# Unit products from GpSimd to VectorE, and a scratch image of whole 32x32 blocks, in the input projection of a two-layer fp32 block

## The chip, the cores and the metric

One core of one Trainium2 chip runs the whole kernel in one launch. The metric is the device time of that launch in microseconds (us). A number of the profile comes from one profiled execution, whose own time stands in the table below.

## The reference, cut to what matters

Two layers over 1280 tokens (256 of context, 1024 latent), everything in fp32, width 1024. Each layer projects the normalised tokens into 23 groups of 128 columns, mixes them, projects back and ends with a mixture of experts. The part that matters here is the mixing of 8 heads of 64 channels by a recurrence, run in both directions:

```python
kk = kk / jnp.maximum(jnp.sqrt(jnp.sum(kk * kk, axis=-1, keepdims=True)), 1e-12)
...
a = jax.nn.sigmoid(iclr_a0[dn] + la @ iclr_a2[dn])
k_dir = k * (1.0 + (a - 1.0) * k_a)
...
s = (s * d_t[:, :, None, :]
     - s_kk[..., None] * (kk_t * a_t)[:, :, None, :]
     + v_t[..., None] * k_t[:, :, None, :])
```

The kernel runs it in chunks of 64 tokens. Within a chunk and head, the steps depend on each other through a triangular 64x64 matrix with ones on its diagonal, which has to be inverted.

## The kernel before, in words

`inproj` does the projection of a layer and, beside it, everything of the recurrence that does not need the running state. The projection is a stream (`project`): per group of 128 columns three matmuls (L397) for each of 8 pieces of the inner dimension and each strip of tokens. The rest is cut into 16 **units**: a pair of heads (e = 0 and 1, 64 partitions each), a half of the tokens (10 chunks), a direction. Per unit:

- `heads` (every second unit): GpSimd spreads the inverse norms over 64 channels (L480), PE turns them by 5 matmuls with the identity (L484), VectorE multiplies (L485).
- `gates`: PE makes two inputs (L502), ScalarE takes tanh (L506), VectorE maps it to the sigmoid by 0.5x+0.5 (L508), a running sum and two exponentials follow.
- `factors`: products of these. The left operand bk of the next step is half GpSimd's work (partitions 64 to 127, L532 and L533) and half VectorE's (L534, L535); the sum over both directions is GpSimd's (L544, L545).
- `attn`: PE multiplies bk with ar (L561), VectorE masks into X (L566). The 64x64 matrices go to a scratch image gD in DRAM (L578), other parts to scratch for the scan (L573, L575). PE transposes bk (L583), ScalarE copies it (L587), and it goes out as well (L589).
- `inverse`, for 3 units at once: the 120 diagonal 32x32 blocks are loaded from gD, one block to a partition, and inverted in place by GpSimd in 30 steps of a product and a sum (L605, L607). ScalarE then makes the transposed blocks zt (L611; L617 and L621 at the end of the layer), and both are stored, to gD (L612, L618) and xD (L622). Units 12 and 13 are inverted on VectorE.
- `merge`: per unit the block inverses come back from gD (L635) and their transposes from xD (L636), and two rounds of PE (L645, L647) and ScalarE (L652, L654) make the missing corner of the 64x64 inverse; the result is stored (L655).

Order: unit u's turn runs merge(u-6), gates(u), attn(u-1), heads, factors(u); after every third unit an inverse is started whose blocks are finished three units later. The class `Pace` puts projection matmuls behind marked PE instructions (`pace.point`), so that PE has work while other engines prepare a unit; a scheduler then fixes the order on every engine. The last merges of a layer run beside the scan (L1061 is the first matmul of a scan step, with st as its tile). All large DMAs are issued by SP, in one order, and each waits for the one eight issues earlier, since eight semaphores are used in turn. So an issue that waits holds up everything behind it.

Of the kernel before, what the change touches and what calls it, by code (L numbers as in the profile page):

```python
# [47 lines left out]
HT, HC = T // 2, NCH // 2  # L48

Q = 32 * C + 32  # L50
U_ = 2 * Q


# [70 lines left out]
class K:  # L124
# [223 lines left out]
    def inproj(self, l, last):  # L348
# [12 lines left out]
        om = sp.tile([P, 15], F32, name="om")  # L361
        nc.vector.tensor_scalar(om, self.vec("mu", 0, 15), -1.0, 1.0, op0=OP.mult, op1=OP.add)
        oka = sp.tile([P, 4], F32, name="oka")
        nc.vector.tensor_scalar(oka, self.vec("ka", 0, 4), -1.0, 1.0, op0=OP.mult, op1=OP.add)
        wah = sp.tile([P, 2, 8], F32, name="wah")
# [17 lines left out]
        def bank():  # L383
            return bk_[0].tile([P, 1024], F32, name="ps1", bufs=bk_[1])
# [92 lines left out]
        def heads(p, hf, k, inv):  # L477

            kk = un.tile([P, HT], F32, name="kk", bufs=2)
# [36 lines left out]

        def factors(p, hf, d, r, k, kk, g, kds):
# [4 lines left out]
            kd = un.tile([P, HC, C], F32, name="kd", bufs=2)  # L522
            nc.scalar.activation(kd, aa, AF.Identity, bias=oka[:, p:p + 1], scale=self.vec("ka", p))
# [6 lines left out]
            bk = un.tile([P, HC, 2, C], F32, name="bk")  # L530
            lo, hi = slice(0, 64), slice(64, 128)
# [11 lines left out]
            if len(kds) == 2:  # L543
                nc.gpsimd.tensor_tensor(kds[0], kds[0], kds[1], op=OP.add)  # L544
                nc.gpsimd.tensor_tensor(kds[0], kds[0], cv(r, hf), op=OP.mult)  # L545
                nc.sync.dma_start(self.prD[p][:, hf * HT:(hf + 1) * HT], flat(kds[0]))
            return ar, bk

        def attn(p, hf, d, ar, bk):

            GR = ((0, 5), (5, 5))
            half = lambda e: slice(64 * e, 64 * e + 64)
            img = slice(hf * HC, (hf + 1) * HC)

            Xs = [un.tile([P, 2, HC, C], F32, name="X", bufs=2) for _ in range(2)]
            for c0, n in ((0, 4), (4, 3), (7, 3)):
                ps = bank().rearrange("q (e c s t) -> q e c s t", e=2, s=2, t=C)
                for c in range(n):
                    for e in range(2):
                        h = half(e)  # L560
                        mm = nc.tensor.matmul(ps[:, e, c], bk[h, c0 + c].rearrange("q s t -> q (s t)"), ar[h, :, c0 + c, :],  # L561
                                              start=True, stop=True)
# [5 lines left out]
            for e in range(2):  # L568
# [3 lines left out]
                for v, rows in ((ar[h], h), (X[o], o)):  # L572
# [3 lines left out]
                                  X[h, 1].rearrange("q (n c) t -> q n (c t)", c=2))  # L576
                m = (2 * place[p, hf, d] + e) * HC
                nc.sync.dma_start(self.mats(self.gD, m, HC), X[h, 0])  # L578

            for c0, n in GR:  # L580
                ps = bank()
# [5 lines left out]
                nc.scalar.activation(bt[:, :n].rearrange("q c t -> q (c t)"), ps[:, :n * P], AF.Copy)  # L587
                ch = slice(hf * HC + c0, hf * HC + c0 + n)
                nc.sync.dma_start(self.btD[d][ch, :, p, :].rearrange("c q x -> q c x"), bt[:, :n])  # L589

        def inverse(u0, n, eng, new=None):
# [4 lines left out]
            else:  # L596
                gt = new()[:n]
                gt, tmp = gt[:, :1024], gt[:, 1024:1280]
            gt = gt.rearrange("q (i a) -> q i a", a=32)
            nc.sync.dma_start(gt, self.diag(self.gD, j0, n))  # L600
            nc.gpsimd.memset(gt.rearrange("q s t -> q (s t)")[:, 0:1024:33], 1.0)
# [6 lines left out]
            def finish():  # L608
                if new is None:
# [3 lines left out]
                else:  # L613
                    xs = [qp.tile([P, 512], F32, name=name)[:n].rearrange("q (a i) -> q a i", i=32)
                          for name in ("pq", "pl")]
                    for x, sl in zip(xs, (slice(0, 16), slice(16, 32))):
                        nc.scalar.activation(x, gt[:, :, sl].rearrange("q i a -> q a i"), AF.Copy)  # L617
                    nc.sync.dma_start(self.diag(self.gD, j0, n), gt)  # L618
                    xt = gt
                    for x, sl in zip(xs, (slice(0, 16), slice(16, 32))):  # L620
                        nc.scalar.activation(xt[:, sl], x, AF.Copy)  # L621
                nc.sync.dma_start(self.diag(self.xD, j0, n), xt)  # L622
            return finish

        def merge(u, new, bank="pq"):
# [7 lines left out]
            for e, (r, o) in enumerate(ro):  # L633
                m = (2 * u + e) * HC
# [357 lines left out]

    @staticmethod
    def mats(t, m, n):

        return bass.AP(tensor=t.tensor, offset=t.offset + m * U_, ap=[[C, C], [U_, n], [1, C]])

    @staticmethod
    def diag(t, b, n):

        return bass.AP(tensor=t.tensor, offset=t.offset + b * Q, ap=[[Q, n], [C, 32], [1, 32]])

# [827 lines left out]
def trace(tc, a, out):  # L1830
# [17 lines left out]
    k.yD = [dram(f"yD{d}", [2, T, 4 * C]) for d in range(2)]  # L1848
    k.gD = dram("gD", [5 * P * Q])
    k.xD = dram("xD", [5 * P * Q])  # L1850
    xs = [a["x0"], dram("x1", [T, D])]
# [90 lines left out]
```

## Time and profile before

| | us |
|---|---|
| runs: median (lowest to highest of 3) | 3627.87 (3625.42 to 3634.18) |
| the profiled execution: its own time | 3623.64 |
| its span on the core | 3621.7 |
| PE, VectorE (DVE), ScalarE (ACT), GpSimd (POOL) busy in it | 3063.4, 2281.6, 1880.5, 1178.0 |

The units of layer 1 lie between about 160 and 640 us of the span, those of layer 2 between about 2010 and 2490. The chain that ended last covers only the last few microseconds, so the stretch is read through what PE waited for. A line number is that of the kernel before; a name such as zt is the program's name of a tile, and `zt<-xD` a load of it.

### The profile page before, as it was taken

The page shows a single profiled execution, that of the slowest core. Times are in us where ns is not written, and L with a number is a line of the kernel's source. Part 1 is how long each engine was busy: PE and PEld are TensorE (multiplying, and loading weights), DVE is VectorE, ACT ScalarE, POOL GpSimd, SP SyncE. Part 2 cuts the span into 40 slices and gives each one's busy share as a digit, 9 for nine tenths or more (in the row PEclk, how much of TensorE's full clock was granted, in tenths as well). Part 3 has the DMA queues.
Part 4 walks back from the last instruction along what each step waited for, and adds up shares of the span by engine and source line. Part 5 has one row for each costly group of instructions (what it writes and reads, how often), then busy time and mean ns, then how long its engine had stood idle before and what let it go on. Part 6 is the DMA issues. An engine that isn't in the chain of part 4 may idle for free. (4 is left out here: it accounts for less than half of the span.)

```text
span 3621.7 us, 59282 instructions
## 1 busy us (share of the span) xinstructions
PE 3063.4 (85%) x22308; PEld 2426.6 (67%) x22308; DVE 2281.6 (63%) x3543; ACT 1880.5 (52%) x2838; POOL 1178.0 (33%) x1101
## 2 busy tenths in 40 slices
PE   6998788888997999999829988778878978999992
PEld 3776666676686777777616766556666857777772
DVE  4265566134487888888672665652334778888886
ACT  4343433335344777778652434323343467777783
POOL 0037675211221222222140276743113122233323
PEclk8998888899998999999959988778988989999996
DMA  6677888879746899999667578889795488899995
GB/s 241 207 167 173 185 192 181 246 230 315 260 142 243 334 339 338 365 373 363 257 227 258 144 169 181 176 180 252 240 285 167 133 315 317 331 366 364 360 366 205
DMA packets 708060, 922.35 MB, mean 255 GB/s; under 512 B 335074, under 2 KB 561259, under 8 KB 657852
## 3 DMA queue, kind: packets, MB, share of 16 engines
q1 hardware_dynamic: 669456, 871.05, 75.8%
q0 software_dynamic: 38304, 47.49, 3.9%
q8 instruction: 177, 2.90, 0.3%
q14 instruction: 111, 0.91, 0.1%
q10 hardware_dynamic: 12, 0.00, 0.0%
HBM read 726.92 MB, written 203.23 MB: 257 GB/s over the span
## 5 line engine op out<-in xcount | busy, mean ns | idle before, releaser
L176 DVE TENSOR_TENSOR hl<-ld,hl 128x1024 fp32r<-128x1024 f32 x734 | 869.2, 1228 | 54.2 <-ACT hl L175 44.2
L175 ACT ACTIVATE hl<-ld 128x1024 fp32r<-128x1024 f32 x796 | 798.5, 1052 | 38.4 <-PE pR L1571 21.9
L1571 PE MATMUL pR<-hl,wk 128*128 128x512 f32 x1560 | 455.1, 400 | 0.0
L1571 PE MATMUL pU<-hl,wk 128*128 128x512 f32 x1560 | 446.9, 395 | 0.0
L397 PE MATMUL pb<-hh,wh 128*128 128x512 f32 (+1 forms) x1000 | 393.0, 394 | 10.2 <-ACT wh L175 5.4
L397 PE MATMUL pb<-hl,wh 128*128 128x512 f32 (+1 forms) x1000 | 389.1, 390 | 0.0
L397 PE MATMUL pb<-hh,wl 128*128 128x512 f32 (+1 forms) x1000 | 385.4, 386 | 0.0
L1595 PE MATMUL pA<-hl,wk 128*128 128x512 f32 x1560 | 382.9, 401 | 0.5 <-ACT wk L175 0.5
L1571 PEld LDWEIGHTS pU<-hl,wk 128*128 128x128 f32 x1560 | 294.5, 189 | 68.3
L1595 PEld LDWEIGHTS pA<-hl,wk 128*128 128x128 f32 x1560 | 292.7, 191 | 64.0 <-ACT wk L175 0.7
L1571 PEld LDWEIGHTS pR<-hl,wk 128*128 128x128 f32 x1560 | 288.3, 189 | 60.7 <-ACT wk L175 0.3
L176 POOL TENSOR_TENSOR hl<-ld,hl 128x1024 fp32r<-128x1024 f32 x62 | 184.2, 2971 | 422.4 <-ACT hl L175 422.4
L397 PEld LDWEIGHTS pb<-hh,wh 128*128 128x128 f32 x1000 | 200.2, 200 | 76.8 <-issue 14.1
L1602 POOL DMA_INDIRECT yb<-wk,sca x64 | 94.8, 1482 | 468.2 <-ACT wk L1601 452.1
L1276 PE MATMUL pA<-hl,wk 128*128 128x512 f32 x864 | 226.6, 413 | 7.7 <-POOL wk L176 4.0
L397 PEld LDWEIGHTS pb<-hl,wh 128*128 128x128 f32 x1000 | 201.1, 201 | 37.9 <-issue 10.3
L397 PEld LDWEIGHTS pb<-hh,wl 128*128 128x128 f32 x1000 | 200.2, 200 | 35.2 <-issue 4.6
L1100 POOL DMA_DIRECT2D yD<-yt x72 | 58.0, 805 | 433.7 <-ACT yt L1099 391.6
L1276 PEld LDWEIGHTS pA<-hl,wk 128*128 128x128 f32 x864 | 163.0, 195 | 49.2 <-issue 6.0
L1088 DVE TENSOR_TENSOR tm<-pR,ST 128x256 f32<-128x256 f32 x76 | 32.1, 423 | 249.4 <-PE pR L1083 237.4
L175 ACT ACTIVATE wk<-pm 128x256 fp32r<-128x256 f32 (+1 forms) x195 | 88.8, 455 | 185.6 <-PE pm L1586 169.3
L607 POOL TENSOR_TENSOR gt<-gt,tmp 120x30 f32<-120x30 f32 (+14 forms) x240 | 168.3, 701 | 17.7
(425 smaller groups left out, 5389.6 us busy)
## 6 DMA issues: line engine op xcount, KB each, us to landing
ld<-in_exp_gu SPq DMA_DIRECT2D x260, 1024.0 KB
ld<-in_exp_dn SPq DMA_DIRECT2D x130, 1024.0 KB
st<-rlD SPq DMA_DIRECT2D x80, 512.0 KB
wr<-in_w_in SPq DMA_DIRECT2D x46, 512.0 KB
rlD<-ar SPq DMA_DIRECT2D x64, 320.0 KB
rlD<-X SPq DMA_DIRECT2D x64, 320.0 KB
btD<-bt SPq DMA_DIRECT2D x64, 320.0 KB
st<-abD SPq DMA_DIRECT2D x40, 512.0 KB
```

Source lines behind the costliest of these rows:

```text
L175: nc.scalar.activation(hi, src, AF.Copy)
L176: (eng or nc.vector).tensor_tensor(lo, src, hi.bitcast(F32), op=OP.subtract)
L397: mm = nc.tensor.matmul(ps[:, :n], w[:, k, :], h[:, k, c0:c0 + n], start=(k == 0 and i == 0), stop=(k == KD - 1 and i == 2))
L607: eng.tensor_tensor(gt[:, 0:j, j + 1:32], gt[:, 0:j, j + 1:32], tv, op=OP.add)
L1088: nc.vector.tensor_tensor(tm, RS[:, 1], ST[d], op=OP.add)
L1100: nc.gpsimd.dma_start(self.yD[d][:, ch * C:(ch + 1) * C, :], yt.rearrange("q p d -> q (p d)"))
L1276: nc.tensor.matmul(ps, oo[o][:, k, :], w[k][w_][:, fs], start=(k == 0 and q == 0), stop=(k == KD - 1 and q == 2))
L1571: nc.tensor.matmul(o, x.xT[xi][:, kk, :], w[wi][:, k, :], start=(kk == 0 and i == 0), stop=(kk == KD - 1 and i == 2))
L1595: nc.tensor.matmul(x.y[n], x.h[:, hi_, f, :], dw[wi][:, 0, n * 512:(n + 1) * 512], start=(f == 0 and i == 0), stop=(f == 3 and i == 2))
L1602: nc.gpsimd.indirect_dma_start(out=yb, out_offset=bass.IndirectOffsetOnAxis(ap=x.sca, axis=0), in_=o, in_offset=None, bounds_check=2 * T - ...
```

## The change

GpSimd keeps only the block inverses. `heads` broadcasts on PE (10 matmuls instead of 5). In `gates` and `factors` the map 0.5x+0.5 of the second gate is folded into what follows, that of the first goes to ScalarE, and all products go to VectorE. bk has three slots instead of two, so that its product kk*a is one instruction over 128 partitions; the transposition of bk by PE becomes 20 plain matmuls with 64 columns instead of 10 transposes with 128. The image gD holds whole 32x32 blocks (4 KB each, contiguous), and the corner blocks lie in another image, nD: `attn` writes three pieces per e instead of one, `inverse` loads and stores its blocks whole. The transposed image xD is gone, with ScalarE's copies and the store; `merge` loads three pieces per e instead of two, and transposes the blocks by 20 matmuls with the identity (L640 of the new kernel) and two copies, ahead of its two rounds.

```diff
@@ heads
-            nc.gpsimd.tensor_copy(kk.rearrange("q (t e d) -> q t e d", e=2, d=64),
-                                 inv[:, 5 * hf:5 * hf + 5, :, None].to_broadcast([P, 5, 2, 64]))
             for t in range(5):
-                nc.tensor.matmul(ps[:, t * P:(t + 1) * P], kk[:, t * P:(t + 1) * P], self.ident, start=True, stop=True)
+                for e in range(2):
+                    nc.tensor.matmul(ps[64 * e:64 * e + 64, t * P:(t + 1) * P],
+                                     inv[:, 5 * hf + t, e:e + 1].to_broadcast([P, 64]), self.ident, start=True, stop=True)
@@ gates
-                nc.vector.tensor_scalar(dst, dst, 0.5, 0.5, op0=OP.mult, op1=OP.add)
+                if i == 0:
+                    nc.scalar.activation(dst, dst, AF.Copy, bias=0.5, scale=0.5)
@@ factors
-            nc.vector.tensor_tensor(aa, aa, Ei, op=OP.mult)
+            nc.vector.scalar_tensor_tensor(aa, aa, 1.0, Ei, op0=OP.add, op1=OP.mult)
...
-            nc.gpsimd.tensor_tensor(bk[hi, :, 0, :], kd[hi], Ei[hi], op=OP.mult)
-            nc.gpsimd.tensor_tensor(bk[hi, :, 1, :], kk[hi, :, rev], aa[hi, :, rev], op=OP.mult)
-            nc.vector.tensor_tensor(bk[lo, :, 1, :], kd[lo], Ei[lo], op=OP.mult)
-            nc.vector.tensor_tensor(bk[lo, :, 0, :], kk[lo, :, rev], aa[lo, :, rev], op=OP.mult)
+            for e in range(2):
+                h = slice(64 * e, 64 * e + 64)
+                nc.vector.tensor_tensor(bk[h, :, 2 - 2 * e], kd[h], Ei[h], op=OP.mult)
+            nc.vector.scalar_tensor_tensor(bk[:, :, 1], kk[:, :, rev], 0.5, aa[:, :, rev], op0=OP.mult, op1=OP.mult)
...
-                nc.gpsimd.tensor_tensor(kds[0], kds[0], kds[1], op=OP.add)
-                nc.gpsimd.tensor_tensor(kds[0], kds[0], cv(r, hf), op=OP.mult)
+                nc.vector.tensor_tensor(kds[0], kds[0], kds[1], op=OP.add)
+                nc.vector.tensor_tensor(kds[0], kds[0], cv(r, hf), op=OP.mult)
@@ attn
-                nc.sync.dma_start(self.mats(self.gD, m, HC), X[h, 0])
+                for b in range(2):
+                    q = slice(32 * b, 32 * b + 32)
+                    nc.sync.dma_start(self.diag(m, b), X[h, 0][q, :, q])
+                nc.sync.dma_start(self.corner(m), X[h, 0][0:32, :, 32:64])
...
-                    mm = nc.tensor.transpose(ps[:, c * P:(c + 1) * P], bk[:, c0 + c].rearrange("q s t -> q (s t)"),
-                                             self.ident)
+                    for e in range(2):
+                        h = half(e)
+                        mm = nc.tensor.matmul(ps[:, e, c], left(e, c0 + c), self.ident[h, h], start=True, stop=True)
@@ inverse, finish
-                    xt = un.tile([P, 32, 32], F32, name="zt")[:n]
-                    nc.scalar.activation(xt, gt.rearrange("q i a -> q a i"), AF.Copy)
-                    nc.sync.dma_start(self.diag(self.gD, j0, n), gt)
...
-                nc.sync.dma_start(self.diag(self.xD, j0, n), xt)
+                nc.sync.dma_start(img, gt.rearrange("q i a -> q (i a)"))
@@ merge
-                nc.sync.dma_start(AM[64 * e:64 * e + 64], self.mats(self.gD, m, HC))
-                nc.sync.dma_start(XP[r], self.mats(self.xD, m, HC)[lo, :, lo])
+                nc.vector.memset(AM[o, :, lo], 0.0)
+                nc.sync.dma_start(AM[r, :, hi], self.corner(m))
+                for b, (rows, cols) in enumerate(((r, lo), (o, hi))):
+                    nc.sync.dma_start(AM[rows, :, cols], self.diag(m, b))
...
+                            nc.tensor.matmul(pq[r, c, :], AM[r, c, lo], self.ident[r, r], start=True, stop=True)
...
+                    nc.scalar.activation(XP[r], pq[r], AF.Copy)
@@ the image
+    def blocks(self, b, n):
+        return bass.AP(tensor=self.gD.tensor, offset=self.gD.offset + b * 1024, ap=[[1024, n], [1, 1024]])
+    def diag(self, m, b):
+        return bass.AP(tensor=self.gD.tensor, offset=self.gD.offset + (2 * HC * m + b) * 1024,
+                       ap=[[32, 32], [2048, HC], [1, 32]])
+    def corner(self, m):
+        return bass.AP(tensor=self.nD.tensor, offset=self.nD.offset + HC * m * 1024, ap=[[32, 32], [1024, HC], [1, 32]])
```

The order of SP around an early merge of layer 1 before, from the X writes of one unit (gD, rlD, abD) to the loads of the merge (zt):

```order
L578 DMA gD<-X 64x10x64
L573 DMA rlD_62<-X 64x10x128
L575 DMA abD_64<-X 64x5x128
L578 DMA gD<-X 64x10x64
L589 DMA btD_66<-bt 128x5x128
L635 DMA zt<-gD 64x10x64
L636 DMA zt<-xD 32x10x32
L589 DMA btD_66<-bt 128x5x128
L635 DMA zt<-gD 64x10x64
L636 DMA zt<-xD 32x10x32
```

The same place after:

```order
L581 DMA gD<-X 32x10x32
L582 DMA nD<-X 32x10x32
L574 DMA rlD_62<-X 64x10x128
L576 DMA abD_64<-X 64x5x128
L581 DMA gD<-X 32x10x32 x2
L582 DMA nD<-X 32x10x32
L595 DMA btD_66<-bt 128x5x128
L630 DMA zt<-nD 32x10x32
L632 DMA zt<-gD 32x10x32 x2
L595 DMA btD_66<-bt 128x5x128
L630 DMA zt<-nD 32x10x32
L632 DMA zt<-gD 32x10x32 x2
```

Between the first X write and the last load of the merge there are now six more issues: four X writes and two loads.

The order of PE at the first merge of layer 1 before (L397 is the projection, L561 the products of `attn`, L645 and L647 the rounds of the merge):

```order
L397 MATMUL pb<-hh,wl 128x256
L645 MATMUL pq<-zt 32x32
L561 MATMUL ps_2765<-ar,bk 128x128 x8
L645 MATMUL pq<-zt 32x32 x19
L561 MATMUL ps_2776<-ar,bk 128x128 x6
L397 MATMUL pb<-hh,wl 128x512
L397 MATMUL pb<-hh,wh 128x512
L397 MATMUL pb<-hl,wh 128x512
L647 MATMUL pq<-zt 32x32 x20
```

The same merge after, in its two pieces. First the transpositions (L640) and what follows them, where L501 is the unit's gates:

```order
L396 MATMUL pb<-hl,wh 128x512
L640 MATMUL pq<-ident,zt 32x32 x20
L501 MATMUL ps_2860<-lw,w_589 128x320 x2
L501 MATMUL ps_2865<-la,a_590 128x320 x2
L396 MATMUL pb<-hh,wh 128x256
L396 MATMUL pb<-hl,wh 128x256
```

Then, ten projection matmuls later, the first round (L650) with `attn` (L562) behind it:

```order
L396 MATMUL pb<-hh,wh 128x256
L396 MATMUL pb<-hl,wh 128x256
L650 MATMUL pq<-zt 32x32 x20
L562 MATMUL ps_2876<-ar,bk 128x128 x8
L562 MATMUL ps_2887<-ar,bk 128x128 x6
```

Before, the merge's first round stood behind the gates, around the products of `attn`; now the transpositions, which wait for the loads, stand ahead of the gates, and `attn` stands behind the first round.

## Rows read from the trace of the kernel before

**Rows 1.** The page: busy time of the engines; granted TensorE clock in 40 slices.

```profile
PE 3063.4 (85%) x22308; PEld 2426.6 (67%) x22308; DVE 2281.6 (63%) x3543; ACT 1880.5 (52%) x2838; POOL 1178.0 (33%) x1101
...
PEclk8998888899998999999959988778988989999996
```

**Rows 2.** Busy time by window (columns as in the header), units of layers 1 and 2.

```profile
160.00:640.00 480.00, 411.60 (x3214) 329.17 (x3214) 288.19 (x392) 186.75 (x264) 283.41 (x343) 0.88 0.80 176
2010.00:2490.00 480.00, 393.07 (x3024) 305.61 (x3018) 280.76 (x389) 178.10 (x258) 287.82 (x358) 0.84 0.82 180
```

**Rows 3.** Waits of PE, layer 1 (160:640): total us, times, longest us.

```profile
PE pq L645 <- DMA zt<-xD: 30.8, 8, 13.4
PE pR L1061 <- DMA st<-vE: 11.8, 1, 11.8
PE ps L561 <- POOL bk L533: 7.6, 3, 3.7
```

**Rows 4.** Waits of PE, layer 2 (2010:2490).

```profile
PE pq L645 <- DMA zt<-xD: 25.8, 10, 6.7
PE ps L561 <- POOL bk L533: 14.3, 4, 5.8
PE pR L1061 <- DMA st<-vE: 12.3, 2, 12.1
```

**Rows 5.** Timeline of PE: start, duration, work, in brackets the idle time before.

```profile
346.20 0.24 PE L645 MATMUL pq<-zt 32*32 32x32 f32 x2 [4.37 <-DMA zt<-xD]
...
444.91 0.28 PE L645 MATMUL pq<-zt 32*32 32x32 f32 x2 [13.37 <-DMA zt<-xD]
...
606.30 0.28 PE L645 MATMUL pq<-X 32*32 32x32 f32 x2 [4.13 <-DMA X<-xD]
...
2376.87 0.31 PE L645 MATMUL pq<-zt 32*32 32x32 f32 x2 [6.75 <-DMA zt<-xD]
```

**Rows 6.** Groups of POOL by shape, layer 1: busy us, mean ns, idle before.

```profile
L533 POOL TENSOR_TENSOR bk<-kk,aa 64x640 f32<-64x640 f32 x16 | 34.1, 2133 | 2.8 <-DVE kk L485 2.5
L532 POOL TENSOR_TENSOR bk<-kd,Ei 64x640 f32<-64x640 f32 x16 | 32.3, 2016 | 43.6 <-PE ps L583 20.9 <-issue 17.2 <-ACT v L430 3.6
```

**Rows 7.** A product of DVE: its group, and its min/median/max ns in 200:560.

```profile
L534 DVE TENSOR_TENSOR bk<-kd,Ei 64x640 f32<-64x640 f32 x16 | 19.3, 1207 | 21.9 <-PE ps L583 21.7
...
L534 DVE TENSOR_TENSOR bk<-kd,Ei x14: 816/932/2170, 206.4 to 538.9; 64x640 f32<-64x640 f32 x14
```

**Rows 8.** Timeline of PE: three starts, each with the start behind it.

```profile
486.89 0.82 PE L645 MATMUL pq<-zt 32*32 32x32 f32 x40
487.64 0.50 PE L397 MATMUL pb<-hh,wh 128*128 128x512 f32 x1
...
650.00 0.68 PE L1074 MATMUL pU<-RH,st 64*64 64x64 f32 x16
650.61 0.50 PE L397 MATMUL pb<-hh,wl 128*128 128x512 f32 x1
...
357.13 0.71 PE L583 MATMUL ps<-ident,bk 128*128 128x128 f32 x5
357.60 0.48 PE L397 MATMUL pb<-hl,wh 128*128 128x512 f32 x1
```

**Rows 9.** Timeline of SP's queue: start and duration of DMA issues.

```profile
356.54 1.54 SPq L578 DMA_DIRECT2D gD<-X  x1
...
365.49 0.62 SPq L636 DMA_DIRECT2D zt<-xD  x1
366.16 0.64 SPq L635 DMA_DIRECT2D zt<-gD  x1
...
585.17 2.08 SPq L622 DMA_DIRECT2D xD<-zt  x1
587.35 4.03 SPq L573 DMA_DIRECT2D rlD<-X  x1
```

**Rows 10.** The DMA view of 320:340: its packet rows.

```profile
q1 hardware_dynamic: 10606, 2.78, 70.2%
```

More of the change, by code (lines that the diff above doesn't have):

```diff
@@ L48 @@
 HT, HC = T // 2, NCH // 2
-Q = 32 * C + 32
-U_ = 2 * Q
 VOFF = {}
@@ L362, in inproj @@
         nc.vector.tensor_scalar(om, self.vec("mu", 0, 15), -1.0, 1.0, op0=OP.mult, op1=OP.add)
+        hka = sp.tile([P, 4], F32, name="hka")
+        nc.vector.tensor_scalar(hka, self.vec("ka", 0, 4), 0.5, None, op0=OP.mult)
         oka = sp.tile([P, 4], F32, name="oka")
-        nc.vector.tensor_scalar(oka, self.vec("ka", 0, 4), -1.0, 1.0, op0=OP.mult, op1=OP.add)
+        nc.vector.tensor_scalar(oka, self.vec("ka", 0, 4), -0.5, 1.0, op0=OP.mult, op1=OP.add)
         wah = sp.tile([P, 2, 8], F32, name="wah")
@@ L477, in heads @@
         def heads(p, hf, k, inv):
-            kk = un.tile([P, HT], F32, name="kk", bufs=2)
-            nc.gpsimd.tensor_copy(kk.rearrange("q (t e d) -> q t e d", e=2, d=64),
-                                 inv[:, 5 * hf:5 * hf + 5, :, None].to_broadcast([P, 5, 2, 64]))
+            kk = un.tile([P, HT], F32, name="kk")
             ps = bank()
             for t in range(5):
-                nc.tensor.matmul(ps[:, t * P:(t + 1) * P], kk[:, t * P:(t + 1) * P], self.ident, start=True, stop=True)
+                for e in range(2):
+                    nc.tensor.matmul(ps[64 * e:64 * e + 64, t * P:(t + 1) * P],
+                                     inv[:, 5 * hf + t, e:e + 1].to_broadcast([P, 64]), self.ident, start=True, stop=True)
             nc.vector.scalar_tensor_tensor(kk, k[:, hf * HT:(hf + 1) * HT], self.vec("kk", p), ps[:, :HT],
@@ L522, in factors @@
             kd = un.tile([P, HC, C], F32, name="kd", bufs=2)
-            nc.scalar.activation(kd, aa, AF.Identity, bias=oka[:, p:p + 1], scale=self.vec("ka", p))
+            nc.scalar.activation(kd, aa, AF.Identity, bias=oka[:, p:p + 1], scale=hka[:, p:p + 1])
             nc.vector.tensor_tensor(kd, kd, cv(k, hf), op=OP.mult)
             kds.append(kd)
-            nc.vector.tensor_tensor(aa, aa, Ei, op=OP.mult)
+            nc.vector.scalar_tensor_tensor(aa, aa, 1.0, Ei, op0=OP.add, op1=OP.mult)
             ar = un.tile([P, 2, HC, C], F32, name="ar")
-            bk = un.tile([P, HC, 2, C], F32, name="bk")
-            lo, hi = slice(0, 64), slice(64, 128)
-            nc.gpsimd.tensor_tensor(bk[hi, :, 0, :], kd[hi], Ei[hi], op=OP.mult)
-            nc.gpsimd.tensor_tensor(bk[hi, :, 1, :], kk[hi, :, rev], aa[hi, :, rev], op=OP.mult)
-            nc.vector.tensor_tensor(bk[lo, :, 1, :], kd[lo], Ei[lo], op=OP.mult)
-            nc.vector.tensor_tensor(bk[lo, :, 0, :], kk[lo, :, rev], aa[lo, :, rev], op=OP.mult)
+            bk = un.tile([P, HC, 3, C], F32, name="bk")
+            for e in range(2):
+                h = slice(64 * e, 64 * e + 64)
+                nc.vector.tensor_tensor(bk[h, :, 2 - 2 * e], kd[h], Ei[h], op=OP.mult)
+            nc.vector.scalar_tensor_tensor(bk[:, :, 1], kk[:, :, rev], 0.5, aa[:, :, rev], op0=OP.mult, op1=OP.mult)
             if d == 0:
@@ L552, in attn @@
             half = lambda e: slice(64 * e, 64 * e + 64)
+            left = lambda e, c: bk[half(e), c, 1 - e:3 - e].rearrange("q s t -> q (s t)")
             img = slice(hf * HC, (hf + 1) * HC)
@@ L560, in attn @@
                         h = half(e)
-                        mm = nc.tensor.matmul(ps[:, e, c], bk[h, c0 + c].rearrange("q s t -> q (s t)"), ar[h, :, c0 + c, :],
+                        mm = nc.tensor.matmul(ps[:, e, c], left(e, c0 + c), ar[h, :, c0 + c, :],
                                               start=True, stop=True)
@@ L576, in attn @@
                                   X[h, 1].rearrange("q (n c) t -> q n (c t)", c=2))
-                m = (2 * place[p, hf, d] + e) * HC
-                nc.sync.dma_start(self.mats(self.gD, m, HC), X[h, 0])
+                m = 2 * place[p, hf, d] + e
+                for b in range(2):
+                    q = slice(32 * b, 32 * b + 32)
+                    nc.sync.dma_start(self.diag(m, b), X[h, 0][q, :, q])
+                nc.sync.dma_start(self.corner(m), X[h, 0][0:32, :, 32:64])
             for c0, n in GR:
-                ps = bank()
+                ps = bank().rearrange("q (e c d) -> q e c d", e=2, d=C)
                 for c in range(n):
-                    mm = nc.tensor.transpose(ps[:, c * P:(c + 1) * P], bk[:, c0 + c].rearrange("q s t -> q (s t)"),
-                                             self.ident)
+                    for e in range(2):
+                        h = half(e)
+                        mm = nc.tensor.matmul(ps[:, e, c], left(e, c0 + c), self.ident[h, h], start=True, stop=True)
                 pace.point(mm, W_ATTN)
                 bt = un.tile([P, 5, P], F32, name="bt", bufs=2)
-                nc.scalar.activation(bt[:, :n].rearrange("q c t -> q (c t)"), ps[:, :n * P], AF.Copy)
+                nc.scalar.activation(bt[:, :n].rearrange("q c (e d) -> q c e d", e=2),
+                                     ps[:, :, :n].rearrange("q e c d -> q c e d"), AF.Copy)
                 ch = slice(hf * HC + c0, hf * HC + c0 + n)
@@ L598, in inverse @@
                 gt, tmp = gt[:, :1024], gt[:, 1024:1280]
+            img = self.blocks(j0, n)
+            nc.sync.dma_start(gt, img)
             gt = gt.rearrange("q (i a) -> q i a", a=32)
-            nc.sync.dma_start(gt, self.diag(self.gD, j0, n))
             nc.gpsimd.memset(gt.rearrange("q s t -> q (s t)")[:, 0:1024:33], 1.0)
@@ L608, in finish @@
             def finish():
-                if new is None:
-                    xt = un.tile([P, 32, 32], F32, name="zt")[:n]
-                    nc.scalar.activation(xt, gt.rearrange("q i a -> q a i"), AF.Copy)
-                    nc.sync.dma_start(self.diag(self.gD, j0, n), gt)
[L613 to L621, printed above, removed]
-                nc.sync.dma_start(self.diag(self.xD, j0, n), xt)
+                nc.sync.dma_start(img, gt.rearrange("q i a -> q (i a)"))
             return finish
@@ L633, in merge @@
             for e, (r, o) in enumerate(ro):
-                m = (2 * u + e) * HC
-                nc.sync.dma_start(AM[64 * e:64 * e + 64], self.mats(self.gD, m, HC))
-                nc.sync.dma_start(XP[r], self.mats(self.xD, m, HC)[lo, :, lo])
-            def work(ctx):
+                m = 2 * u + e
+                nc.vector.memset(AM[o, :, lo], 0.0)
+                nc.sync.dma_start(AM[r, :, hi], self.corner(m))
+                for b, (rows, cols) in enumerate(((r, lo), (o, hi))):
+                    nc.sync.dma_start(AM[rows, :, cols], self.diag(m, b))
+            def work(ctx):
+                pq = qp.tile([P, 512], F32, name=bank)[:, :HC * 32].rearrange("q (u t) -> q u t", t=32)
+                for c in range(HC):
+                    for r, o in ro:
+                        with ctx:
+                            nc.tensor.matmul(pq[r, c, :], AM[r, c, lo], self.ident[r, r], start=True, stop=True)
+                        ctx = nullcontext()
+                for r, o in ro:
+                    nc.scalar.activation(XP[r], pq[r], AF.Copy)
                 for st in range(2):
@@ L991, in fill @@
         next(tail, None)
[L993 to L1001, printed above, removed]
+    def blocks(self, b, n):
[5 more added lines that the diff above has]
+        return bass.AP(tensor=self.nD.tensor, offset=self.nD.offset + HC * m * 1024, ap=[[32, 32], [1024, HC], [1, 32]])
     def scan(self, l, last):
@@ L1848, in trace @@
     k.yD = [dram(f"yD{d}", [2, T, 4 * C]) for d in range(2)]
-    k.gD = dram("gD", [5 * P * Q])
-    k.xD = dram("xD", [5 * P * Q])
+    k.gD = dram("gD", [64 * HC * 1024])
+    k.nD = dram("nD", [32 * HC * 1024])
     xs = [a["x0"], dram("x1", [T, D])]
```

## The prediction

> **What bounds the kernel now.** I read the page's busy times first. PE is busy 85% of the span, and its granted clock is often 9 or 8 tenths rather than full [rows 1]. An engine that full sets the time of its stretches, but a busy PE at a low clock or a waiting PE still leaves something to win. The change touches the units alone, so I read their two stretches by window: of 480 us in each, PE is busy 411.60 and 393.07, and idle for the other 68 and 87; its clock is 0.88 and 0.84 [rows 2]. VectorE is at 60%, ScalarE at 39%, GpSimd at 59%, and the DMA engines at 80%: none of them is full, and the question is only where one of them ends last.
>
> PE's waits answer it. Most of the idle time is the merge's first round waiting for its last load, 30.8 us in layer 1 and 25.8 in layer 2; then comes the start of the scan, 11.8 and 12.3; GpSimd's half of bk is only 7.6 and 14.3 [rows 3, 4]. Single waits show two kinds of merge wait: four long ones (13.37, 6.75, 4.37, 4.13), which stand where an inverse's blocks go out, and many short ones [rows 5]. Without the three long ones at zt, that is 24.5, the others take 56.6 - 24.5 = 32 us in 15 waits, 2.1 us each. So GpSimd's products have a price of 22 us at most, and the waits beside the inverses' traffic one of 28.6.
>
> **GpSimd's products.** They go: the two largest groups alone are 34.1 and 32.3 us of layer 1 [rows 6]. PE's waits for them, 7.6 + 14.3 = 21.9, can vanish [rows 3, 4]. VectorE is next in the chain, with 64-row products of 1207 ns on average [rows 7] in place of GpSimd's 2016 and 2133 [rows 6], two of them now being in sequence with what it did anyhow. I take three quarters, **-16**, between -22 and 0. VectorE's load grows little: per unit it loses two maps, and gains the second half of one product for bk and one product for the kd sums, while its half of kk*aa grows to 128 rows. With 40% of its time free [rows 2] I cost that at nothing; the same for ScalarE, which gains one map per unit and two small copies per merge, and loses the large transposing copies (61% free). Their cover is PE's stream; if it were gone, each step of a unit would be later by about one product, 1 us, which is inside the bound of 0 above.
>
> First the row: the same product of 64x640 takes 816 ns at best, 932 in the median and 2170 at worst [rows 7], so something outside it stretches it at times. The Trainium skill (SBUF — State Buffer, "Who interferes with whom") says that a VectorE instruction with two SBUF inputs and a GpSimd instruction that reads SBUF share a port, and that the later one waits for the whole of the earlier. By that rule VectorE's products would fall to their 816 ns where GpSimd is silent, and the inverses would take longer beside VectorE's added products. In the sum it would be 16 x (1207 - 816) ns = 6 us per layer on VectorE, which is off the path: nothing by either. No run here shows yet which engine gives way.
>
> **The inverse's traffic.** Gone are the transposed image's store, ScalarE's transposition before it, and the scattered rows of the block load and store. At the end of one inverse the store of xD holds SP's queue 2.08 us, and the next issue 4.03 [rows 9]. In 320:340, a stretch with one such exchange, 10606 packets take 70.2% of 16 engines for 20 us, 21 ns each [rows 10]. Before, an image crosses three times per inverse in rows of 128 bytes, 120 x 32 x 3 = 11520 packets, or 15 us of all 16 engines by these 21 ns; whole blocks need 240 large packets. Of the four long waits (28.6 us [rows 5]) I take **-26**, between -29 and 0.
>
> **The merge's loads.** Between a unit's first X write and the merge's last load, SP issues six more DMAs than before (the order rows above). An issue takes 0.62 to 0.64 us there, for a small piece as for a large one [rows 9]; so the last load can be late by 6 x 0.63 = 3.8 us. Queued behind it on SP are the next unit's stores and the projection's weights. Against this, whole blocks free the engines on which these loads wait. PE's order decides what is seen of it: the transpositions now stand ahead of the gates, and two to four dozen projection matmuls behind the unit before, which cover part. I take **+18**, 1 us for each of 18 merges with zt (9 per layer), between 0 and 18 x 3.8 = +68.
>
> **PE's extra work.** Nearest rows, at full clock: 40 matmuls of 32x32 in 0.75 us (486.89 to 487.64), 16 of 64 columns in 0.61 (0.038 each), 5 of 128 columns in 0.47 (0.094 each) [rows 8]. Per layer: the merge's transpositions, 16 x 0.75 = 12.0; bk's, 16 x (40 x 0.038 - 10 x 0.094) = 9.3, as a plain fp32 matmul runs as two; the broadcast, 8 x 10 x 0.094 = 7.5. That is 29 per layer, 58 in both, and 58 / 0.86 = 67 at the clock of these stretches. It lies in the stretch that PE bounds, but PE idles 155 us there, partly where these small matmuls stand. I take somewhat under a half, **+26**, between 0 and +67.
>
> **The end of a layer.** The last inverses stand ahead of the scan's loads in SP's queue, and PE waits 11.8 and 12.3 us there [rows 3, 4]. With the transposed image gone, I take 5 us of each, **-10**, between -20 and 0.
>
> **The clock.** It fell where PE waited. One hundredth more over the 805 us in which PE is busy [rows 2] is 805 x 0.01 / 0.86 = 9: **-9**, between -20 and +10.
>
> **Sum**: -16 - 26 + 18 + 26 - 10 - 9 = -17. The profiled execution took 3623.6; that makes 3606.6, and the runs' median lies 4.2 above the profiled one: **3611 us**, 0.5% faster. About 0.3% (11 us) is what a measurement of this kernel can tell from no change.
>
> **The rivals.**
>
> *The merge's chain takes over (slower).* Every merge now goes X write, SP's longer queue, loads, transposition on PE, copy on ScalarE, first round: one trip more, and PE stands still in order while it waits. Its place is L640, ahead of the gates and of `attn`, so the wait delays the unit that follows too. It decides from (16 + 26 + 10 + 9 - 26) / 18 = 1.9 us more per merge, or 4 us instead of 2.1. At 3.4 more, close to the 3.8 of six issues, and with no gain of clock, the time is 3628 - 16 - 26 - 10 + 61 + 26 = **3663**. For it speak the waits that exist already, and that small DMAs cost SP as much as large ones [rows 9]. Against it, part of the wait comes from the bursts that go. The Trainium skill (DMA: Bandwidth & Descriptors, "Measured") calls transfers under 64 KB descriptor-dominated, and every new piece is 40 KB: by that rule the pieces cost what whole ones did, which is this rival. The two issue times of rows 9 agree with it, at 0.62 and 0.64 us for 40 and 160 KB. Chance **0.30**.
>
> *PE's extra work is paid in full (no change).* PE is the bound and its small matmuls hide nowhere: 3628 - 16 - 26 - 10 - 9 + 67 = **3634**; somewhat fewer merge waits bring it to the 3628 of before. For it speaks PE's 85%, against it PE's idle time beside the merges. Chance **0.22**.
>
> *The waits go altogether (much faster).* Both GpSimd's (-22) and all long (-29) and short ones (-32) vanish, the end of the layer gains 20, and half of PE's work is hidden (+29): 3628 - 74 = **3554**. For it speaks that traffic falls by some 15 us of DMA time per inverse; against it the six issues. Chance **0.13**.
>
> *The change does not do what it says*: GpSimd's instructions really go, by the order of the program, so I give this nothing.
>
> **Numbers.** The forecast has 0.35. Faster by over 0.3% is the forecast and the third rival, 0.48; within 0.3% the second, 0.22; slower the first, 0.30. The range goes from the third rival's 3554 to the first's 3663, which leaves half of each outside, 0.21. Cases of both signs hold most of the chance; the forecast's own range is 3595 to 3622.
>
> **What would show it.** Right: waits of L561 for bk under 6 us in both layers; no merge wait over 5 us; L640's waits at about 3 us each; VectorE busy within 15 us of before in each window; DMA share of the windows under 0.75. Wrong: L640 waiting over 4 us on average makes the first rival; PE busy up by 30 us or more in each window, with idle time unchanged, the second. A wait of PE for VectorE's bk as large as that for GpSimd's was would strike the first term.

## The result and the profile after

The changed kernel takes 3737.31 us (median of four runs, 3734.57 to 3739.27), the kernel before 3626.64 in the same session: a ratio of 1.0302, interval 1.0284 to 1.0320. It is 111 us slower. The forecast was 3611, with a range up to 3663.

The page of the changed kernel, the two rows that answer to [rows 1]:

```profile
PE 3156.8 (84%) x24708; PEld 2505.0 (67%) x24708; DVE 2259.7 (60%) x3609; ACT 1903.1 (51%) x2910; POOL 972.4 (26%) x989
...
PEclk8998778899998999999959987777987989999996
```

PE is busy for 93 us more, while GpSimd has 206 us less to do. The windows from the first product of `attn` to the first matmul of the scan, now 512 and 508 us long instead of 444.5 and 448.2 (first starts of L561 and L1061 in the trace before, of L562 and L1070 after), in the columns of [rows 2]. Before:

```profile
194.00:638.00 444.00, 376.36 (x3019) 301.79 (x3017) 267.49 (x368) 170.69 (x244) 275.86 (x336) 0.88 0.85 185
2026.00:2475.00 449.00, 363.10 (x2783) 282.56 (x2781) 259.94 (x362) 163.78 (x234) 270.40 (x335) 0.83 0.83 179
```

After:

```profile
191.00:703.00 512.00, 426.03 (x4050) 343.33 (x4049) 255.77 (x397) 178.91 (x273) 182.15 (x294) 0.84 0.63 149
2078.00:2587.00 509.00, 398.84 (x3815) 312.56 (x3813) 251.41 (x391) 173.34 (x265) 184.52 (x295) 0.82 0.63 149
```

These two stretches hold 128 us of loss; 13 come back between the scan of layer 1 and the units of layer 2. PE's busy time in the stretches grew by 49 and 36 us, its idle time by 19 and 24, and its clock fell from 0.88 and 0.83 to 0.84 and 0.82. The DMA engines went from a share of 0.85 and 0.83 to 0.63: the traffic was relieved as meant. Waits of PE in the units of layer 1 of the changed kernel (total us, times, longest), against [rows 3]:

```profile
PE pq L640 <- DMA zt<-gD: 17.8, 12, 3.3
PE ps L501 <- DVE kk L484: 15.6, 3, 10.0
PE ps L501 <- ACT bt L592: 15.5, 2, 10.9
PE pR L1070 <- DMA st<-vE: 13.6, 1, 13.6
```

The same for layer 2, against [rows 4]:

```profile
PE pq L640 <- DMA zt<-gD: 32.2, 10, 11.1
PE pq L650 <- ACT zt L643: 24.0, 4, 21.8
PE pl L675 <- ACT bt L678: 17.3, 3, 15.3
PE pR L1070 <- DMA st<-vE: 11.1, 1, 11.1
```

The wait for GpSimd's bk is gone from both lists, as forecast, and the merges wait 50.0 us for their loads (before 56.6). But new waits have come, for ScalarE's zt and bt and VectorE's kk, with single waits of 21.8, 15.3, 10.9 and 10.0 us. What stands behind the longest one shows on the timelines of GpSimd, SP's queue, ScalarE, VectorE and PE of the changed kernel:

```profile
2286.55 0.24 POOL L614 TENSOR_TENSOR gt<-gt,tmp 120x30 f32<-120x30 f32 x1
...
2286.82 0.34 SPq L616 DMA_DIRECT2D gD<-gt  x1
2287.26 0.62 SPq L443 DMA_DIRECT2D zs<-v  x1
2287.93 1.53 SPq L444 DMA_DIRECT2D zs<-v  x1
...
2292.38 1.36 ACT L453 ACTIVATE v<-v,om 128x1280 f32<-128x1280 f32 x1 [23.18 <-DMA zs<-v]
2293.64 0.72 ACT L513 ACTIVATE E<-sg 128x640 f32<-128x640 f32 x1
2294.27 0.72 ACT L514 ACTIVATE Ei<-sg 128x640 f32<-128x640 f32 x1
2294.90 0.85 ACT L643 ACTIVATE zt<-pq 32x320 f32<-32x320 f32 x2
...
2293.77 1.55 DVE L454 SCALAR_TENSOR_TENSOR v<-zs,vt,v 128x1280 f32<-128x1280 f32 x1 [23.38 <-ACT v L453]
...
2295.80 1.28 PE L650 MATMUL pq<-zt 32*32 32x32 f32 x40 [21.78 <-ACT zt L643]
```

GpSimd ends its inverse at 2286.79. Only then can SP issue the store of the blocks (L616), and behind it in SP's one queue stand the loads of zs, which need no inverse. ScalarE has waited 23.18 us for them, VectorE 23.38 us for ScalarE, PE 21.78 us for the copy that stands behind in ScalarE's order. The store's waits over the whole run, in SP's waits before:

```profile
SPq L612 <- POOL gt L607: 18.9, 5, 4.6
```

And in those of the changed kernel, where the second row is the inverse that VectorE makes:

```profile
SPq L616 <- POOL gt L614: 98.0, 8, 20.2
...
SPq L616 <- DVE lw L614: 19.8, 2, 13.2
```

The order had shown this without a time. Counted in issues on SP's queue in the traces, the store of the inverse stands behind its load, for the four large inverses of layer 1 and of layer 2:

| kernel | layer 1 | layer 2 |
|---|---|---|
| before | 48, 57, 53, 57 | 44, 52, 62, 47 |
| changed | 35, 36, 34, 35 | 31, 28, 36, 35 |
| changed, one-pass transposes (below) | 53, 36, 58, 60 | 45, 64, 58, 54 |

The counts in the expectations below are lower, by up to 12. They fit a count of the order in which issues of one kind in a row stand as one line (x2), which leaves out most where the new image writes and loads its pieces in pairs.

### The profile page after: what moved, and what is told of

The parts are those of the page before. It is cut to its first block, busy times and chain, and to the rows that moved or that the text cites. A ratio compares the mean times of both kernels' runs of the same rounds, so it can differ in the third digit from the quotient of the medians.

```text
span 3737.5 us, 64278 instructions
## 1 busy us (share of the span) xinstructions
PE 3156.8 (84%) x24708; PEld 2505.0 (67%) x24708; DVE 2259.7 (60%) x3609; ACT 1903.1 (51%) x2910; POOL 972.4 (26%) x989
## 5 line engine op out<-in xcount | busy, mean ns | idle before, releaser
L172 DVE TENSOR_TENSOR wk<-pm,wk 128x256 fp32r<-128x256 f32 (+1 forms) x195 | 99.5, 510 | 113.5 <-ACT wk L171 113.2
```

The source lines that it names most:

```text
L172: (eng or nc.vector).tensor_tensor(lo, src, hi.bitcast(F32), op=OP.subtract)
```

## The experiments

All medians are set beside the kernel before, run in the same sessions (3623 to 3629 us). "Stretch" is that from the first product of `attn` to the scan in the profiled execution, both layers added: 892.7 us before, 1020.4 after the change.

**1. The products alone.** Before, with `heads`, `gates` and the products as changed; bk in two slots:

```diff
             bk = un.tile([P, HC, 2, C], F32, name="bk")
...
+            for e in range(2):
+                h = slice(64 * e, 64 * e + 64)
+                nc.vector.tensor_tensor(bk[h, :, 1 - e], kd[h], Ei[h], op=OP.mult)
+                nc.vector.scalar_tensor_tensor(bk[h, :, e], kk[h, :, rev], 0.5, aa[h, :, rev], op0=OP.mult, op1=OP.mult)
```

> The kernel before with GpSimd's products alone moved (broadcast on PE, maps folded, all products on VectorE; bk keeps two slots, its halves as four 64-row products; image, inverse and merge as before). Theory of the store (SP's queue stands still at the store of the block inverses, which now stands about 30 issues behind its load in place of 50): here it stands 42, 47 and 39 issues behind, so a small loss at most, 3610 to 3650 us. Rival, VectorE cannot carry the products: most of the 110 us, 3690 us or more.

3604.65 us, ratio 0.9940 (0.9919 to 0.9961): faster by 23 us (stretch 863.2). VectorE carries the products; the rival falls.

**2. The image alone.** Before, with the changed `inverse`, `merge`, writes of X and addresses, and nothing else:

```diff
-                nc.sync.dma_start(self.mats(self.gD, m, HC), X[h, 0])
...
+                    nc.sync.dma_start(self.diag(m, b), X[h, 0][q, :, q])
+                nc.sync.dma_start(self.corner(m), X[h, 0][0:32, :, 32:64])
...
-                nc.sync.dma_start(XP[r], self.mats(self.xD, m, HC)[lo, :, lo])
...
+                nc.vector.memset(AM[o, :, lo], 0.0)
...
+                            nc.tensor.matmul(pq[r, c, :], AM[r, c, lo], self.ident[r, r], start=True, stop=True)
```

> The kernel before with the image alone changed (whole blocks, corners apart, transpositions of the merge on PE; products stay on GpSimd, bk's transposes as before). Theory of the store: it stands 48, 44 and 48 issues behind its load, so the large waits stay away; only the merges' PE work (about 24 us at full clock in both layers) and the memset wait are paid: 3630 to 3670 us. Rival, the merge's longer chain is what costs: 3690 us or more.

3600.45 us, ratio 0.9921 (0.9899 to 0.9943): faster by 27 us, where I had expected a small loss. In the profiled executions, which are 15 us apart, 9 us lie in the stretch (883.6). So the merge's longer chain and its PE work are paid for. PE's waits for the merges' loads in this run:

```profile
PE pq L635 <- DMA zt<-gD: 26.6, 15, 7.2
```

Half of the 56.6 us before. Both halves gain, so the loss lies in what neither has, bk's third slot and the plain matmuls that transpose it, or in the two halves together, which 5 decides.

**3. The store by GpSimd's queue.**

```diff
-                nc.sync.dma_start(img, gt.rearrange("q i a -> q (i a)"))
+                (nc.gpsimd if eng is nc.gpsimd else nc.sync).dma_start(img, gt.rearrange("q i a -> q (i a)"))
```

> The changed kernel with one edit: the store of the block inverses is issued by GpSimd's own queue, behind the inverse, in place of SP's. Theory of the store: SP's wait of 98 us for the inverses goes, and with it PE's long waits behind zs, bt and vE (21.8, 15.3, 10.9 and smaller ones): 3680 to 3705 us. Rival, PE's extra work alone: within 10 us of the changed kernel's 3737.

3695.31 us, ratio 1.0189 (1.0163 to 1.0215): 42 us less than the changed kernel (stretch 972.9). The order of SP's other issues stayed: 2090 of its 2096 stand in the same order. So SP's standing still is a cause, but of less than half.

**4. The zeroing later.** The memset of the merge's tile moved behind the first round in the program:

```diff
-                nc.vector.memset(AM[o, :, lo], 0.0)
...
                         if st == 0:
+                            nc.vector.memset(AM[o, :, lo], 0.0)
```

> The changed kernel with one edit: VectorE's zeroing of the merge's tile is issued when the first round is done, not ahead of the loads, so that VectorE does not stand still for the tile's former store. Theory of the memset (VectorE waited 48 and 47 us for it in the two layers, and PE 10.0 us and 4.3 us for VectorE behind it): 3705 to 3725 us. Rivals (store, PE's work): within 10 us of 3737.

3735.30 us, ratio 1.0303 (1.0280 to 1.0327): no change. It says little, since the scheduler put the memset back to where it waits, as VectorE's waits in this run show:

```profile
DVE zt L656 <- DMA abD<-zt: 35.1, 6, 11.2
...
DVE zt L656 <- DMA gD<-X: 25.4, 3, 17.4
...
DVE zt L656 <- DMA abD<-X: 17.1, 1, 17.1
```

**5. The old transposes.** The changed kernel with experiment 1's bk and the transposes of before: both halves together, without the plain matmuls.

```diff
-                    for e in range(2):
-                        h = half(e)
-                        mm = nc.tensor.matmul(ps[:, e, c], left(e, c0 + c), self.ident[h, h], start=True, stop=True)
+                    mm = nc.tensor.transpose(ps[:, c * P:(c + 1) * P], bk[:, c0 + c].rearrange("q s t -> q (s t)"),
+                                             self.ident)
```

> The changed kernel with one part undone: bk keeps two slots (its halves by four 64-row products) and PE transposes it by 10 transposes of 128 columns per unit, in place of 20 plain matmuls; products, image and merge as changed. New theory, from the two halves being 0.6 and 0.8 percent faster than before: the loss comes with the plain matmuls, which cost PE time and make the scheduler set the inverse's store too early (here it stands 47, 56 and 47 issues behind its load, in the changed kernel 32, 32 and 29): 3570 to 3605 us. Rival, the two halves spoil each other: 3680 us or more.

3578.97 us, ratio 0.9872 (0.9852 to 0.9893), stretch 845.9. The two halves nearly add up, 44 us of 23 and 27, and the plain matmuls' part is all of the loss and more.

**6. The plain matmuls without the image.** Experiment 1 with three slots and the plain matmuls (edit 5 in reverse; image, inverse and merge as before).

> The products on VectorE and the three slots with plain matmuls, but image, inverse and merge as before. Theory of the plain matmuls: the store stands 31, 29 and 27 issues behind its load, so SP waits for it again and the loss is there without the image: 3680 to 3740 us. Rival, the image and the matmuls only together: about the 3605 of the products alone plus some 25 us of PE work, 3630 us.

3757.05 us, ratio 1.0358 (1.0337 to 1.0379). From 3605 to 3757 by these matmuls and their slot; SP's wait for the inverse comes back with them, without the new image:

```profile
SPq L618 <- POOL gt L613: 98.2, 7, 21.3
```

**7. One word in the changed kernel.** The same 20 operations, slots and layout, but as transposes, which run in one pass instead of two:

```diff
-                        mm = nc.tensor.matmul(ps[:, e, c], left(e, c0 + c), self.ident[h, h], start=True, stop=True)
+                        mm = nc.tensor.transpose(ps[:, e, c], left(e, c0 + c), self.ident[h, h])
```

> The changed kernel with the 20 plain matmuls per unit as 20 transposes of the same shape (64 columns), one pass each; three slots stay. Theory of the plain matmuls: the store stands 47, 31 and 47 issues behind its load, and PE runs 20 instructions in place of 40: 3580 to 3640 us. Rival, the slots' layout or the number of instructions costs: 3700 us or more.

3579.22 us, ratio 0.9863 (0.9841 to 0.9885): 158 us less than the changed kernel and level with 5, so the slot with its layout costs nothing on balance and the kind of instruction everything. On PE's timeline of the changed kernel, a start of the group and the start behind it:

```profile
224.96 1.23 PE L589 MATMUL ps<-ident,bk 64*128 64x64 f32 x20
226.12 1.95 PE L466 MATMUL pl<-hsel,v 128*128 128x2 f32 x16
```

The same with one-pass transposes:

```profile
224.30 0.47 PE L589 MATMUL ps<-ident,bk 64*128 64x64 f32 x10
224.70 0.50 PE L396 MATMUL pb<-hh,wh 128*128 128x512 f32 x1
```

20 instructions of the plain form take 1.16 us, 0.058 each; 10 of one pass take 0.40, 0.040 each, and there are half as many: 0.116 against 0.040 us per block, almost a factor of three. (Most groups at the full clock take 0.058 to 0.063 and 0.040 to 0.046.) The Trainium skill (TensorE: Matmul & The Clock Gate, "Terms") calls the transpose mode four times as fast for FP32; the trace agrees in kind, at a smaller factor. Per layer the group is busy 46.3 and 49.0 us as plain matmuls, 17.5 and 19.3 as transposes: 58.5 us in both, not 158. The group in the changed kernel, layer 1 and layer 2:

```profile
L589 PE MATMUL ps<-ident,bk 64*128 64x64 f32 x640 | 46.3, 295 | 4.1 <-DVE lw L614 4.1
L589 PE MATMUL ps<-ident,bk 64*128 64x64 f32 x640 | 49.0, 303 | 4.0 <-DVE X L567 4.0
```

And with one-pass transposes:

```profile
L589 PE MATMUL ps<-ident,bk 64*128 64x64 f32 x320 | 17.5, 236 | 10.6 <-DVE X L567 10.3 <-DVE inv L471 0.3
L589 PE MATMUL ps<-ident,bk 64*128 64x64 f32 x320 | 19.3, 256 | 0.0
```

The rest is order and clock: the stretches shrink by 145 us (to 445.9 and 429.5), of which 82 are busy and 63 idle time of PE, the clock in them is 0.88 and 0.85, and SP's wait for the inverses falls from 98.0 to 33.6 us, as its view in this run has it:

```profile
SPq L616 <- POOL gt L614: 33.6, 3, 15.2
```

The three waits follow the table: the stores that stand 36, 45 and 53 issues behind wait 15.2, 12.3 and 6.2 us, those 54 or more behind do not wait.

**8. The same with the store by GpSimd's queue, on the old transposes** (edits 5 and 3).

> As the run with the old transposes, and the store of the block inverses issued by GpSimd's queue. Theory of the store: where it stands late enough, SP hardly waits for it, so little is left to win: within 12 us of that run. Rival, the store's wait on SP costs at any place: another 20 us or more.

3572.91 us, ratio 0.9844 (0.9825 to 0.9863): overlaps with 5. Where the store stands late, moving it wins little or nothing.

**9 and 10. More PE time by cheap instructions.** The transposes of 7, each issued two or three times (below twice):

```diff
-                        mm = nc.tensor.transpose(ps[:, e, c], left(e, c0 + c), self.ident[h, h])
+                        for _ in range(2):
+                            mm = nc.tensor.transpose(ps[:, e, c], left(e, c0 + c), self.ident[h, h])
```

> The kernel with one-pass transposes of 64 columns (3579 us), each issued twice: 640 in a layer's units, as many PE instructions as the plain matmuls made. Theory of PE's own time: 640 x 0.055 = 35 us against 46 per layer for the plain ones, so 17.5 x 2 = 35 us of PE more than 3579, at the clock of the stretch 40: 3620 us. Theory of the plan: the scheduler puts the stores 47, 30, 29, 48 and 39, 45, 48, 42 issues behind their loads, so the long waits stay away in layer 2: 3600 to 3640 us. If the number of PE instructions alone makes the loss: 3700 us or more.

> The same, each transpose issued three times: 960 per layer, some 52 us of PE against the 46 of the plain matmuls, but with the stores 36, 30, 28, 39 and 39, 47, 46, 43 issues behind their loads. If PE's time makes the loss of 158 us between 3579 and 3737, this is at 3737 or above; if the plan makes most of it, 3579 + 2 x 35 / 0.86 = 3660 us, between 3630 and 3690.

3628.22 us (0.9997, 0.9983 to 1.0010) and 3656.42 us (1.0072, 1.0046 to 1.0098). Three times means 960 instructions per layer, busy 42.2 and 41.0 us, nearly the plain matmuls' 46.3 and 49.0 and in more instructions, yet 81 us faster than the changed kernel. Their group in layer 1 and layer 2:

```profile
L590 PE MATMUL ps<-ident,bk 64*128 64x64 f32 x960 | 42.2, 247 | 13.4 <-DVE X L567 7.8 <-DVE lw L615 5.5
L590 PE MATMUL ps<-ident,bk 64*128 64x64 f32 x960 | 41.0, 240 | 9.8 <-DVE X L567 5.7 <-DVE lw L615 4.0
```

So neither the number of PE instructions nor its time alone makes the loss. What PE's time costs shows in the stretches of the two layers, 461.7 and 444.0 us with two, 490.6 and 445.9 with three: for each microsecond that the group is busy longer than in 7, they are 1.8 and 1.4 us longer with two, 1.8 and 0.8 with three. The 0.8 is layer 2, where the stores stand 45 to 58 issues behind and SP waits only 3.3 us for them; in layer 1 three of the four stand 35 to 39 behind, and it waits 43.8 us. By these ratios the plain matmuls' 58.5 us would cost 47 to 105 of the 145 us of the stretches (an estimate: the order moves here too).

**11. Half of the plain matmuls**: the first group of five chunks plain, the second as transposes.

```diff
-                        mm = nc.tensor.matmul(ps[:, e, c], left(e, c0 + c), self.ident[h, h], start=True, stop=True)
+                        if c0:
+                            mm = nc.tensor.transpose(ps[:, e, c], left(e, c0 + c), self.ident[h, h])
+                        else:
+                            mm = nc.tensor.matmul(ps[:, e, c], left(e, c0 + c), self.ident[h, h], start=True, stop=True)
```

> The same kernel with the first group of five chunks by plain matmuls and the second by one-pass transposes: half of the disputed part. PE's time alone: half of 59 us, 3610 us. The plan, in which the stores stand 47, 29, 28, 41 and 39, 44, 31, 40 issues behind: 3620 to 3680 us. All by halves: 3658 us.

3649.13 us, ratio 1.0062 (1.0041 to 1.0083): 70 of the 158 us, near to a half (stretch 937.6, 62 of the 145).

**12. One-pass transposes and the store by GpSimd's queue** (edits 7 and 3).

> The one-pass transposes of 64 columns, and the store of the block inverses from GpSimd's queue: the version that should be fastest. SP waited 33.6 us for the inverses without it: 3560 to 3579 us by the theory of the store; without it 3579.

3605.81 us, ratio 0.9940 (0.9921 to 0.9959): slower than 7, against both theories. The units' stretch is no longer (874.4 us against 875.4); what differs in the profiles is layer 2 from the scan to the experts' first matmul, 463.5 us against 443.5. Why is open. In the traces of all these kernels that part takes 441 to 464 us, in no order that follows the edits (459.9 before, 463.4 after the change). So a difference of 20 us between two medians can come from there, and what an edit does to the units is read from the stretch.

**13 and 14. No wait for the zeroing.** In the changed kernel ScalarE zeroes, from a bank that it has just read; 14 has the store by GpSimd's queue too.

```diff
-                nc.vector.memset(AM[o, :, lo], 0.0)
...
                             nc.scalar.activation(XP[o], pq[o], AF.Copy)
+                            nc.scalar.activation(AM[o, :, lo], pq[o], AF.Copy, scale=0.0)
```

> The changed kernel with the zeroing of the merge's tile on ScalarE, from the first round's bank times zero, behind the copy that reads the same bank: VectorE no longer waits for the tile's former store, and the stores of the inverses stand where they stood (32, 31, 30, 30 issues). Theory of the zeroing: PE's waits for VectorE's kk (15.6 us) go, with part of those for bt: 3705 to 3725 us. Rival, VectorE's wait is hidden behind SP's: 3730 to 3745 us.

> The same with the store of the inverses from GpSimd's queue. If zeroing and store are two separate costs: some 20 us below the 3695 of the store alone, 3665 to 3685 us. If what is left is PE's time and the rest of the order: 3685 to 3705 us.

3712.08 us (1.0241, 1.0205 to 1.0277) and 3691.51 us (1.0181, 1.0154 to 1.0208). The stretches are 994.9 and 971.3. The zeroing costs 25 us by itself, but only 4 of them are left, within the intervals, once the store is off SP: the two waits cover each other. With both gone, the stretch is 49 us shorter, and some 64 us over before remain.

**15 and 16. The same zeroing where the order is sound**, on 7 and on 8.

> The kernel with one-pass transposes of 64 columns (3579 us) and the zeroing on ScalarE. Theory of the zeroing: 10 to 20 us less, 3559 to 3569 us. Rival: 3570 to 3590 us.

> The kernel with the old transposes and the store from GpSimd's queue (3573 us), and the zeroing on ScalarE. Theory of the zeroing: 3553 to 3563 us. Rival: 3565 to 3585 us.

3562.64 us (0.9810, 0.9778 to 0.9842) and 3572.94 us (0.9854, 0.9816 to 0.9891). The first is the fastest of all, 1.9% under the kernel before, though its interval touches that of 7; the second equals 8.

## Why the prediction was wrong

**GpSimd's products (-16): right in kind.** The waits of 21.9 us vanished, and no wait for VectorE's bk took their place at `attn`; the part alone gained 23 us, 29.5 in the stretch. The row that I weighed with the Trainium skill (SBUF — State Buffer, "Who interferes with whom") went the way of its rule: with GpSimd's own products gone, VectorE's product is at 888 ns on average, from 1207 [rows 7]. The longer inverses that I also took from it did not come: the operations of an inverse in layer 1 are busy 35.5 to 41.2 us, before 36.5 to 42.5. VectorE's group in layer 1 after:

```profile
L533 DVE TENSOR_TENSOR bk<-kd,Ei 64x640 f32<-64x640 f32 x32 | 28.4, 888 | 10.7 <-PE ps L589 10.4
```

**The inverse's traffic (-26) and the merge's loads (+18): the gain was right, the loss not.** The image alone, with the merges' PE work, gained 27 us (9 in the stretch), and the merges waited 26.6 us in it, from 56.6. In the changed kernel L640 waits 50.0 us in 22 waits, 2.3 each, under the 4 us that I had named as the slower rival's sign (though one of them is 11.1, where I had said that none would pass 5). The 3.8 us that I put on six more issues per merge did not show; so my slower rival had the right sign by a wrong mechanism, and the rule beside it on transfers under 64 KB (the Trainium skill, DMA: Bandwidth & Descriptors, "Measured") decided nothing here.

**PE's extra work (+26): mis-sized at bk's transposition.** Here a term of the sum failed. I had set 9.3 us per layer for it, with 0.038 us per instruction from a row whose weights are 64 columns wide [rows 8]. The plain matmuls have weights of 128 columns and take 0.058 to 0.063; measured by busy time the group grew by 21.0 and 20.6 us per layer (46.3 - 25.3 and 49.0 - 28.4). Its rows before, layer 1 and layer 2:

```profile
L583 PE MATMUL ps<-ident,bk 128*128 128x128 f32 x160 | 25.3, 292 | 0.2
L583 PE MATMUL ps<-ident,bk 128*128 128x128 f32 x160 | 28.4, 321 | 9.7 <-DVE X L566 9.7
```

And I took over half of all of it as hidden in PE's idle time, while doubling or trebling cheap transposes made the stretches 0.8 to 1.8 us longer for each microsecond that they were busy. That fits a chain in which PE's work lies in front of the others; which link carries it was not tested. The sign that I had named for the second rival came in part: PE is busy for 49 and 36 us more, but its idle time grew as well, and that rival's full price of +67 ends at 3634.

**The end of a layer (-10) and the clock (-9): wrong.** The scan's first wait is 13.6 and 11.1 us, from 11.8 and 12.3 [rows 3, 4]. The clock fell from 0.88 and 0.83 to 0.84 and 0.82, while PE's idle time grew by 19 and 24 us.

**What the sum did not have: the order.** The step that failed most is the one that took each instruction's cost and left the order around it as it was. My sum has no term for it. A scheduler makes the order, and the plain matmuls moved the inverse's store from 44 to 62 issues behind its load to 28 to 36. SP's queue then stood still for 98.0 us, from 18.9, and with it loads that have nothing to do with the inverse. That the instruction's kind moves the store is shown by experiment 7, which changes nothing else; that the scheduler holds plain fp32 matmuls for slower than they are, and so plans more time for the inverse per issue, is argued only. I had the order of both kernels and looked in it for the merge's loads, not for what stands behind an issue that waits for GpSimd.

How the 158 us split is settled in part. In the profiled executions, which are 154 apart, 145 lie in the stretches. There the store and the zeroing take 49 together (experiment 14; all but some 120 of SP's 2096 other issues keep their order in it), and by proportion to experiment 10 PE's time takes 47 to 105. What the order of other work adds lies between, and stays open.

## What to carry to other kernels

Where a scheduler sets the order, read in it, before pricing an edit, what stands behind each issue that waits for a slow engine, in one queue that all loads share: here a store some 20 issues too early cost 42 us, more than the new image gained. Transpose by the one-pass instruction and not by a plain fp32 matmul with the identity: here this alone was 158 us. When a change of several parts loses, run its parts alone: here two parts of three were gains that the third one hid.

## What the runs showed of the hardware

A plain fp32 matmul with weights of 64x128 and 64 columns takes 0.058 to 0.063 us in a row at the full clock, the one-pass transposition of the same shape 0.040 to 0.046, and the plain one comes twice; before, a transposition of 128x128 took 0.094 [rows 8]. Without GpSimd's products among them, the 60 operations of an inverse of 120 blocks end 40 to 46 us after the first, in layer 1, instead of 57 to 62.
